# A two-block transformer kernel on one core: 256-byte lines, four query heads at a time, a third raw panel buffer, and five moves in the order of work

## The chip, the cores and the metric

The kernel runs on one core of one Trainium2 chip. The metric is device time in microseconds (us) of one execution; lower is better. TensorE (PE) does the matmuls, VectorE (DVE) and ScalarE (ACT) the elementwise work, GpSimd (POOL) a few small operations, and all DMAs are issued from SyncE's queue (SP).

## The reference

Everything is float32. `first_block` runs two layers over 512 tokens of width 1024. Each layer has a mixing part and a feed-forward part:

```python
h = rmsnorm(x, g_pre_mix[l])
(c_q, c_kv, k_r, p_in, s_u, s_v, cv_b, cv_c, cv_x, gate_logits) = split_cols(h @ w_in[l])
y_a = mla_branch(c_q, c_kv, k_r, ...) @ w_br_a[l]      # 8 heads, latent attention
y_b = pool_branch(p_in, ...) @ w_br_b[l]
y_c = sgu_branch(s_u, s_v, ...) @ w_br_c[l]
y_d = conv_branch(cv_b, cv_c, cv_x, ...) @ w_br_d[l]
merged = sum of sigmoid(gate_logits)[branch] * y_branch
x = x + rmsnorm(merged @ w_out[l], g_post_mix[l])
h = rmsnorm(x, g_pre_ffn[l])
x = x + rmsnorm((silu(h @ w_ffn_gate[l]) * (h @ w_ffn_up[l])) @ w_ffn_down[l], g_post_ffn[l])
```

`second_block` runs one layer: a modulated norm, neighbourhood attention with 8 heads, a gated linear attention in both directions (which also reads 256 context tokens), output gates, a merge, `w_out`, and a feed-forward part of the same shape.

## The kernel before

**Matmuls.** A float32 product is made of three matmuls in the fp32r type: `split` casts an operand into a high part on ACT (L261) and makes the low part, the rest, on DVE (L262), and `mm3` (L309) adds high x high, high x low and low x high in one PSUM bank. In the trace `wh` and `wl` are the two parts of a weight panel, `hTh` and `hTl` those of the transposed activations, `ah`/`al`, `mTh`/`mTl`, `brh`/`brl`, `oTh`/`oTl` those of other operands. In `out<-a,b` the first input is the one that streams, the second the one that is loaded as weights.

**Weight panels.** `panel` (L273) loads 128 x 1024 floats with one DMA into a raw buffer `wr` (two of them, `WR`), then splits it into `wh` and `wl` (four of each, `WH`). A raw buffer is free again when its `wl` is made; a `wh`/`wl` pair when the last matmul that reads it is done. Where four panels are used for all four token tiles in turn (`tm`, L574, called with the list that `pans` makes), a new set of four can be split only as the last tile releases the old set.

**Order.** TensorE's order is the program's: `inorder` (L245) chains every matmul to the one before. The other engines' order is made by the tile framework's scheduler from the program order and its own estimate of when inputs are ready; each engine then runs its list strictly in order, the DMA queue as well. Side work is woven in by hand: `beside` (L188) takes a list of items, and a `tick` (L153), twice per full matmul group, runs one step of it; `later(f, n)` runs `f` at the n-th tick from then.

**PSUM.** The eight banks are tagged `g` (3), `s` (2), `tp` (2), `po` (1). The main thread takes `g` for everything, side work takes `s` for products and `tp` for transposes.

**SBUF.** Pools are stacks, one growing from the left and one from the right. `Aligned.tile` (L100) rounds a tile's row up to a multiple of 128 bytes, so a tile may start at an odd multiple of 128. In the first block a pool `const1` stays open under all stage pools on the left; its tiles of 34, 4, 12 and 8 floats take 256 + 128 + 128 + 128 = 640 bytes, an odd number of 128-byte lines, and its one other tile 2048. It is closed before the second block.

**Places that the change touches.**
- `mla` (L735): `queries(hp, t2)` projects two heads for two token tiles: 12 matmuls of 192 columns (L764), four head transposes and a copy. There are eight calls per layer. `keys` and `scores` go by pairs of heads; the item list is at L831.
- `sgu_branch`: `turned` (L944) transposes two groups of four 128 x 128 tiles into `g` banks, and `split` empties them.
- `ffn_up` (L479): six panels lead, two of them made ahead of time. They run on the first 256 tokens while the pending transposes of token tiles 2 and 3 (`flush`) are placed after panels 1 and 3. The four other leading panels' `wl` are queued on DVE behind the split of tile 1.
- `block2` (L1114): neighbourhood queries, then the gated linear attention's inputs (panel set at column 1536), context tiles, the set at 2048, the sets for neighbourhood keys (512) and values (1024), and then four panels at 2560 for the output gates `og` (L1183), each made just before its matmuls. `on_v` issues eight DMAs per token tile.
- `normed` (L1496): the norm of neighbourhood queries and keys; its transposes come three ticks later.
- `norm` (L350) of the context tiles, and `decays` (L1277), take scratch tiles of their own.

Of the kernel before, what the change touches and what calls it, by code (L numbers as in the profile page):

```python
# [24 lines left out]
EPS = 1e-6  # L25
NEG = -1e30
HEADS = 8
WR, WH = 2, 4
F2 = {"g": 4, "a": 4}
LEAD = 6  # L30
TURN = 2
# [7 lines left out]
WIN0 = (0, 8, 24, 32)  # L39
CTX = 256  # L40
PHASE = 0
WARM = 12
HIGH = ((0, 0), (1, 0), (0, 1))

# [49 lines left out]
class Aligned:  # L94
# [5 lines left out]
    def tile(self, shape, dt, **kw):  # L100
        size = 2 if dt == BF16 else 4
        n = math.prod(shape[1:])
        if n * size % P == 0:
            return self.pool.tile(shape, dt, **kw)
        line = P // size
        t = self.pool.tile([shape[0], -(-n // line) * line], dt, **kw)[:, :n]
        if len(shape) == 2:
            return t
        names = "abc"[: len(shape) - 1]
        spaced = " ".join(names)  # L110
        return t.rearrange(f"p ({spaced}) -> p {spaced}", **dict(zip(names[1:], shape[2:])))


class Builder:
# [232 lines left out]
        lo = pool.tile([P, KD, n], F32R, name=self.nm("hTl"), tag="hTl")  # L347
        return hi, lo

    def norm(self, q, x, g, b=None, after=None):  # L350

        nc = self.nc
        ms = self.small(1)
        j = q.tile([P, D], BF16, name=self.nm("jk"), tag="jk")
        self.queue(nc.scalar.activation(j, x, AF.Square, scale=D ** -0.5, accum_out=ms), after)  # L355
        r = self.rstd(ms, 1)
        hns = []
        for h in range(2):
            c = slice(h * 512, h * 512 + 512)
            hn = q.tile([P, 512], F32, name=self.nm("hn"), tag="hn", bufs=4)  # L360
# [118 lines left out]
    def ffn_up(self, hT, before, wg, wu, ks, rs):  # L479
        nc = self.nc  # L480
        acts = []
        jobs = [(i, w) for i in range(NFF) for w in (wg, wu)]
        pans = self.ahead + [self.panel(w, 0, KD, i * P, P, after=self.turned_at[1] if i < 2 else None) for i, w in jobs[len(self.ahead) : LEAD]]
        banks = [self.bank(x) for x in ("g", "g", "g", "po", "s", "s")]

        def part(n, h):
            ts = slice(h * 256, h * 256 + 256)
            if n == h == 0:
                ls, rs = ([(x[0][:, k, c], x[1][:, k, c]) for k in range(KD)] for x, c in ((pans[0], slice(P)), (hT, ts)))
                return self.mm3s(banks[0][:, ts], ls, rs, HIGH)  # L490
            for k in range(KD):
                self.mm3(banks[n][:, ts], (pans[n][0][:, k], pans[n][1][:, k]), (hT[0][:, k, ts], hT[1][:, k, ts]), k == 0, k == KD - 1)

        for n in range(LEAD):
            part(n, 0)
            if n in (1, 3):
                self.flush()
        for n in range(LEAD):
            part(n, 1)
        before.close()  # L500
        keep = self.pool("actk", 1, stack=ks)
        drop = self.pool("actd", 1, stack=rs, side="right")
# [232 lines left out]
    def mla(self, l, o, q, kv):  # L735
# [19 lines left out]
        def queries(hp, t2):  # L755
            if t2 == 0:
                wqs[hp] = self.panel(a["w_uq"][l], 0, 2, hp * 192, 192)
                qTs[hp] = q.tile([QK, 2, SEQ], F32, name=self.nm("qT"), tag="qT", bufs=2)
            wq, qT = wqs[hp], qTs[hp]
            ps = self.ps()  # L760
            for i in range(2):
                ts = slice((2 * t2 + i) * P, (2 * t2 + i) * P + P)
                for k in range(2):
                    self.mm3(ps[:, i * 192 : i * 192 + 192], (cT[0][:, k, ts], cT[1][:, k, ts]), (wq[0][:, k], wq[1][:, k]), k == 0, k == 1)  # L764
            four = lambda x, d: x.rearrange("p (t h d) -> p t h d", t=2, h=2)
            v = four(ps[:, :384], QK)
            qn = self.f2()
            qv = four(qn[:, :384], QK)
            nc.scalar.activation(qv[:, :, :, :64], v[:, :, :, :64], AF.Copy, scale=QK ** -0.5)
            rt = self.f2()  # L770
            ra, rb = four(rt[:, :128], ROPE), four(rt[:, 128:256], ROPE)
            tab = lambda x, lo, hi: x[:, 2 * t2 : 2 * t2 + 2, None, lo:hi].to_broadcast([P, 2, 2, hi - lo])
            nc.vector.tensor_tensor(ra, v[:, :, :, 64:96], tab(Cq, 0, 32), op=ALU.mult)
            nc.vector.tensor_tensor(rb[:, :, :, :16], v[:, :, :, 80:96], tab(Sq, 0, 16), op=ALU.mult)
            nc.vector.tensor_tensor(rb[:, :, :, 16:], v[:, :, :, 64:80], tab(Sq, 16, 32), op=ALU.mult)
            nc.vector.tensor_tensor(qv[:, :, :, 64:96], ra, rb, op=ALU.add)

            def turn():
                pt = self.ps("t")
                for i in range(4):  # L780
                    self.transpose(pt[:QK, i * P : i * P + P], qv[:, i // 2, i % 2], ident)
                nc.scalar.copy(qT.rearrange("p h (t n) -> p t h n", t=NT)[:, 2 * t2 : 2 * t2 + 2], pt[:QK].rearrange("p (t h n) -> p t h n", t=2, h=2))

            pTs["q", hp, t2] = turn

        def keys(hp):
            wk = self.panel(ukv, 0, 1, hp * 256, 256)
# [9 lines left out]
        def scores(hp, j):  # L797
            n = (j + 1) * P
            ps = []
            for i in range(2):  # L800
                s = self.ps()
                self.matmul(s[:, :n], qTs[hp][:, i, j * P : j * P + P], kTs[hp][:, i, :n], start=True, stop=True)
# [22 lines left out]
        def do(f, *args):  # L825
            return lambda: f(*args)

        def project(hp):
            return [[do(queries, hp, t2), lambda: None, lambda t2=t2: pTs.pop(("q", hp, t2))()] for t2 in range(2)] + [[do(keys, hp)]]

        items = [[do(values, t)] for t in range(NT)] + project(0) + [[]]  # L831
        for hp in range(4):
            more = project(hp + 1) if hp < 3 else []
            for j in range(NT):
                items.append([do(scores, hp, j), lambda: None, do(probs, hp, j), do(values_of, hp, j)])
                if more:
                    items.append(more.pop(0))
        return items

    def softmax(self, q, s, n, bufs):  # L840
# [64 lines left out]
    def sgu_branch(self, l, w_in, hT, brp, q):  # L905
# [37 lines left out]

        def turned():  # L944
            for m in range(2):
                pt = self.ps("t")
                for t in range(NT):
                    self.transpose(pt[:, t * P : (t + 1) * P], cs[:, t, m * P : (m + 1) * P], ident)
                self.split(cT[0][:, m], cT[1][:, m], pt)
# [164 lines left out]
    def block2(self, hT, before):  # L1114
# [24 lines left out]
        with ExitStack() as st:  # L1139
            tmp = self.pool("ctx", 1, stack=st, side="right")  # L1140
            A, B = self.mod_rows(2)(tmp, "ga"), self.mod_rows(5)(tmp, "gb")
            with self.thread("a"):
                for t in range(2):
                    xc = tmp.tile([P, D], F32, name=self.nm("xc"), tag=f"xc{t}")
                    nc.sync.dma_start(xc, a["ctx_2"][0, t * P : (t + 1) * P])
                    hns = self.norm(tmp, xc, A, B)
# [21 lines left out]
        for name, c0 in (("k", 512), ("v", 1024)):  # L1168
            pans = self.pans(w_in, c0)
            for h, n, nt in ((hcT, name + "c", 2), (hT, name, NT)):  # L1170
                for t in range(nt):
                    ps = self.tm(h, pans, t, 512)
                    with self.thread("a"):
                        na[n](t, ps)
        self.drain()
# [4 lines left out]
        og = [q.tile([P, SEQ], F32, name=self.nm("og"), tag=f"og{m}") for m in range(4)]  # L1180
        self.beside(self.gla_outputs(gla, og, zT, q), 1)
        for m in range(4):
            ps = self.fm(hT, self.panel(w_in, 0, KD, 2560 + m * P, P), 0)  # L1183
            nc.scalar.activation(og[m], ps, AF.Tanh, scale=0.5)
            nc.vector.scalar_tensor_tensor(og[m], og[m], 1.0, ps, op0=ALU.add, op1=ALU.mult)
            nc.vector.tensor_scalar(og[m], og[m], gla["gain"], 0.5, op0=ALU.mult, op1=ALU.mult)
# [43 lines left out]
    def gla_project(self, hT, q, cq):  # L1230
# [46 lines left out]
        def decays(tmp):  # L1277

            jobs = [(zc, t, lac) for t in range(2)] + [(zT, t, la) for t in range(NT)]
            es, ds = ([tmp.tile([P, 512], F32, name=self.nm("g" + x), tag=f"g{x}{i}") for i in range(6)] for x in "ed")  # L1280

            def finish(i):
                t, dst = jobs[i][1:]
# [198 lines left out]
    def na_project(self, q):  # L1482
# [13 lines left out]
        def normed(ps, turned):  # L1496
# [15 lines left out]
            self.later(turn, 3)  # L1512

        def on_k(t, ps):
            dst = kT[:, :2048].rearrange("p (i n) -> p i n", i=4)[:, :, t * P : t * P + P]
# [150 lines left out]
```

## Time and profile before

| | us |
|---|---|
| median of 3 runs | 2477.08 (2476.04 to 2478.45) |
| the profiled execution's own time | 2477.62 |
| its span, first to last instruction | 2475.8 |
| mean granted TensorE clock | 0.996 of full |

| engine | busy us | share | instructions |
|---|---|---|---|
| PE | 2450.2 | 99% | 12155 |
| weight loads (PEld) | 2017.2 | 81% | 12155 |
| DVE | 1232.1 | 50% | 2018 |
| ACT | 851.2 | 34% | 1414 |
| POOL | 73.4 | 3% | 113 |

Matmuls are pipelined: one is listed with 0.39 us, but the next starts long before that. What a matmul costs is the distance from its start to the next one's start, and a stretch with a known number of matmuls shows how much of it was lost.

### The profile page before, as it was taken

To read this page: it belongs to the slowest core of one execution; us is meant where nothing else is said; L and a number is where in the kernel's file an instruction comes from. 1 tells how busy PE (TensorE), PEld (TensorE's weight loads), DVE (VectorE), ACT (ScalarE), POOL (GpSimd) and SP (SyncE) were. 2 spreads that over 40 slices of the span, in tenths; PEclk is the share of its full clock that TensorE was granted. 3 is DMA by queue.
4 is the path that set the end of the run, shared out by engine and by line. 5 is a ranking of instruction groups with operands and counts; after the bars stand their busy time and mean duration, and the time that the engine had idled before them with its cause. 6 is when DMAs were issued, how large, how long until landed. Compare 5 with 4: busy or idle time off the path is not lost.

```text
span 2475.8 us, 30539 instructions
## 1 busy us (share of the span) xinstructions
PE 2450.2 (99%) x12155; PEld 2017.2 (81%) x12155; DVE 1232.1 (50%) x2018; ACT 851.2 (34%) x1414; POOL 73.4 (3%) x113
## 2 busy tenths in 40 slices
PE   9999999999999999999999999999999999999999
PEld 7877788988888887778898888877877778988887
DVE  6456544566522645554455443275535646543323
ACT  4343433322322434343332222244434533322211
POOL 1000000000000100000000000020100000000000
PEclk9999999999999999999999999999999999999999
DMA  5323334345424432443435333451133225333323
GB/s 160 92 75 110 105 94 153 119 136 174 134 94 141 128 96 79 123 124 94 153 111 154 101 96 104 141 179 48 55 94 120 69 69 170 111 94 97 99 94 128
DMA packets 339376, 279.72 MB, mean 113 GB/s; under 512 B 28262, under 2 KB 282430, under 8 KB 339233
## 3 DMA queue, kind: packets, MB, share of 16 engines
q1 hardware_dynamic: 339233, 277.76, 37.6%
q8 instruction: 96, 1.57, 0.3%
q14 instruction: 47, 0.39, 0.0%
HBM read 262.27 MB, written 15.45 MB: 112 GB/s over the span
## 4 chain that ended last, share of the span: by engine, by line
PE 61%; DVE 3%; ACT 1%; issue 1%; DMA 1%; POOL 0%; DVEq 0%; ACTq 0%; POOLq 0%; SPq 0%
PE pg L252 47%; PE ps L252 6%; PE ppo L252 3%; PE ptp L252 3%; PE ptp L255 2%; DVE wl L262 1%; DMA wr<-in_w_mod 1%; ACT wh L261 0%; POOL sm L337 0%; DVE hn L361 0%; ACT p L847 0%; DVE xt L412 0%; DVE hTl L262 0%; ACT jk L355 0%; DMA wr<-in_w_ffn_up 0%
## 5 line engine op out<-in xcount | busy, mean ns | idle before, releaser
L262 DVE TENSOR_TENSOR wl<-wr,wh 128x1024 fp32r<-128x1024 f32 (+1 forms) x392 | 463.6, 1184 | 739.2 <-ACT wh L261 719.1
L261 ACT CAST wh<-wr 128x1024 fp32r<-128x1024 f32 (+1 forms) x392 | 398.9, 1020 | 1063.3 <-issue 394.4
L252 PE MATMUL pg<-hTh,wh 128*128 128x512 f32 x1760 | 693.7, 394 | 3.2 <-ACT wh L261 2.1
L252 PE MATMUL pg<-hTh,wl 128*128 128x512 f32 x1760 | 682.3, 388 | 0.3 <-DVE wl L262 0.3
L252 PE MATMUL pg<-hTl,wh 128*128 128x512 f32 x1760 | 681.6, 387 | 0.0
L252 PEld LDWEIGHTS pg<-hTh,wh 128*128 128x128 f32 x1760 | 331.3, 188 | 75.5 <-issue 6.4
L252 PEld LDWEIGHTS pg<-hTh,wl 128*128 128x128 f32 x1760 | 331.1, 188 | 69.8 <-DVE wl L262 1.1
L252 PEld LDWEIGHTS pg<-hTl,wh 128*128 128x128 f32 x1760 | 331.5, 188 | 67.4 <-issue 2.4
L252 PE MATMUL pg<-wh,hTh 128*128 128x512 f32 (+2 forms) x288 | 113.6, 396 | 1.2 <-ACT wh L261 1.2
L252 PE MATMUL pg<-wl,hTh 128*128 128x512 f32 (+2 forms) x288 | 110.9, 387 | 3.3 <-DVE wl L262 3.3
L337 POOL TENSOR_TENSOR sm<-sm,misc 128x1 f32<-128x1 f32 (+3 forms) x72 | 58.8, 819 | 1745.2 <-DVE sm L336 1032.2
L252 PE MATMUL pg<-wh,hTl 128*128 128x512 f32 (+2 forms) x288 | 110.1, 384 | 0.0
L512 DVE TENSOR_TENSOR f<-f,pg 128x512 f32<-128x512 f32 x60 | 41.2, 686 | 122.0 <-PE pg L252 121.9
L1078 DVE SCALAR_TENSOR_TENSOR f<-wr,misc,f 128x512 f32<-128x512 f32 x112 | 81.3, 747 | 29.6 <-DMA wr<-in_w_mod 29.1
L847 ACT ACTIVATE p<-ps,sm 128x512 f32<-128x512 f32 (+3 forms) x96 | 55.7, 580 | 89.6 <-DVE sm L844 89.6
L252 PE MATMUL pg<-wh,al 128*128 128x512 f32 x198 | 77.3, 390 | 0.0
L252 PE MATMUL pg<-wl,ah 128*128 128x512 f32 x198 | 77.3, 390 | 0.0
L252 PE MATMUL pg<-wh,ah 128*128 128x512 f32 x198 | 77.3, 390 | 0.0
L252 PEld LDWEIGHTS pg<-wl,hTh 128*128 128x128 f32 x288 | 54.5, 189 | 16.2 <-DVE wl L262 6.0
L252 PEld LDWEIGHTS pg<-wh,hTh 128*128 128x128 f32 x288 | 54.5, 189 | 12.4 <-ACT wh L261 2.1
L252 PEld LDWEIGHTS pg<-wh,hTl 128*128 128x128 f32 x288 | 54.5, 189 | 10.2
L859 ACT COPY pT<-ptp 128x512 f32<-128x512 f32 (+3 forms) x96 | 41.5, 484 | 50.3 <-PE ptp L255 50.2
(361 smaller groups left out, 3605.7 us busy)
## 6 DMA issues: line engine op xcount, KB each, us to landing
wr<-in_w_in SPq DMA_DIRECT2D x128, 512.0 KB
wr<-in_w_ffn_gate SPq DMA_DIRECT2D x66, 512.0 KB
wr<-in_w_ffn_up SPq DMA_DIRECT2D x66, 512.0 KB
wr<-in_w_ffn_down SPq DMA_DIRECT2D x66, 512.0 KB
wr<-in_w_mod SPq DMA_DIRECT2D x96, 256.0 KB
wr<-in_w_out SPq DMA_DIRECT2D x24, 512.0 KB
xd<-xt SPq DMA_DIRECT2D x20, 512.0 KB
xt<-xd SPq DMA_DIRECT2D x20, 512.0 KB
```

The lines of the kernel that those rows point to most:

```text
L252: self.inorder(self.nc.tensor.matmul(*args, **kw))
L255: self.inorder(self.nc.tensor.transpose(*args, **kw))
L261: h = (copy or nc.scalar.copy)(hi, src)
L262: l = nc.vector.tensor_tensor(lo, src, hi.bitcast(F32), op=ALU.subtract)
L337: nc.gpsimd.tensor_tensor(r, r, self.mhalf[:, :n], op=ALU.pow)
L512: nc.vector.tensor_tensor(t, t, ps, op=ALU.mult)
L847: nc.scalar.activation(p[:, :n], s[:, :n], AF.Exp, bias=nm, accum_out=sm)
L859: self.nc.scalar.copy(pT[:, :n], tp[:, :n])
L1078: nc.vector.scalar_tensor_tensor(acc, raw, sc, acc, op0=ALU.mult, op1=ALU.add)
```

## The change

- `WR` goes from 2 to 3: a third raw panel buffer.
- `LINE = 256`: tiles are rounded up to 256 bytes instead of 128.
- `queries` takes four heads and one token tile per call: 6 matmuls of 384 columns. There are still eight calls per layer; `qT` is twice as large. The item list is rearranged: keys of pair 1 in the first pair's scores, queries of heads 4 to 7 and keys of pair 2 in the second's, keys of pair 3 in the third's.
- `sgu_branch.turned` takes `tp` banks.
- `ffn_up`: only four leading panels at first; the other two after the first `flush`, with their `wl` queued behind the split of token tile 2.
- `block2`: the four output-gate panels are asked for after the matmuls of the last value tile.
- Neighbourhood queries' transposes come five ticks later instead of three; keys keep three.
- The context norm writes over its input, the sixth `ds` tile of `decays` is taken from the thread's scratch buffers, and the DMA scratch is 512 instead of 1024.

```diff
-WR, WH = 2, 4
+WR, WH = 3, 4
+LINE = 256
...
-        if n * size % P == 0:
+        if n * size % LINE == 0:
...
-        line = P // size
+        line = LINE // size
...
-        pans = self.ahead + [self.panel(w, 0, KD, i * P, P, after=self.turned_at[1] if i < 2 else None) for i, w in jobs[len(self.ahead) : LEAD]]
+        pans = list(self.ahead)
+
+        def more(n):
+            for i, w in jobs[len(pans) : n]:
+                pans.append(self.panel(w, 0, KD, i * P, P, after=self.turned_at[1]))
+
+        more(LEAD - 2)
...
             if n in (1, 3):
                 self.flush()
+                more(LEAD)
...
-            for i in range(2):
-                ts = slice((2 * t2 + i) * P, (2 * t2 + i) * P + P)
-                for k in range(2):
-                    self.mm3(ps[:, i * 192 : i * 192 + 192], (cT[0][:, k, ts], cT[1][:, k, ts]), (wq[0][:, k], wq[1][:, k]), k == 0, k == 1)
+            for k, w in enumerate(wqs[f]):
+                self.mm3(ps[:, :384], (cT[0][:, k, ts], cT[1][:, k, ts]), (w[0][:, 0], w[1][:, 0]), k == 0, k == 1)
...
-        items = [[do(values, t)] for t in range(NT)] + project(0) + [[]]
+        items = [[do(values, t)] for t in range(NT)] + project(0) + [[do(keys, 0)], []]
+        more = [[[do(keys, 1)]], project(1) + [[do(keys, 2)]], [[do(keys, 3)]], []]
...
-                pt = self.ps("t")
+                pt = self.bank("tp")
...
                     ps = self.tm(h, pans, t, 512)
+                    if n == "v" and t == NT - 1:
+                        pans = [self.panel(w_in, 0, KD, 2560 + m * P, P) for m in range(4)]
...
-            ps = self.fm(hT, self.panel(w_in, 0, KD, 2560 + m * P, P), 0)
+            ps = self.fm(hT, pans[m], 0)
...
-            normed(ps, turned)
+            normed(ps, turned, 5)
```

## Rows read from the trace of the kernel before

**Rows 1.** The page, part 1: busy us, share, instructions of each engine.
```profile
PE 2450.2 (99%) x12155; PEld 2017.2 (81%) x12155; DVE 1232.1 (50%) x2018; ACT 851.2 (34%) x1414; POOL 73.4 (3%) x113
```

**Rows 2.** The page, part 4: the chain that ended last, shares by engine.
```profile
PE 61%; DVE 3%; ACT 1%; issue 1%; DMA 1%; POOL 0%; DVEq 0%; ACTq 0%; POOLq 0%; SPq 0%
```

**Rows 3.** Timeline of PE (start, us, instruction): a query burst, a value burst.
```profile
106.91 0.25 PE L252 MATMUL ps<-wh,cTh 128*128 128x192 f32 x1
...
108.23 0.42 PE L252 MATMUL pg<-hTh,wh 128*128 128x512 f32 x1
...
62.19 0.28 PE L252 MATMUL ps<-wh,cTh 128*128 128x256 f32 x1
...
62.90 0.39 PE L252 MATMUL pg<-hTh,wh 128*128 128x512 f32 x1
```

**Rows 4.** Groups by form, PE (count, busy us, mean ns, idle): two gate products.
```profile
L252 PE MATMUL pg<-brl,wh 128*128 128x512 f32 x96 | 37.8, 394 | 0.0
...
L252 PE MATMUL pg<-oTl,wh 128*128 128x512 f32 x96 | 37.3, 389 | 0.0
```

**Rows 5.** Timeline of PE: one down projection, before and after its operands change pool.
```profile
772.51 0.39 PE L252 MATMUL ps<-wh,ah 128*128 128x512 f32 x1
...
794.28 0.40 PE L252 MATMUL ps<-wh,ah 128*128 128x512 f32 x1
...
808.92 0.40 PE L252 MATMUL ptp<-wh,ah 128*128 128x512 f32 x1
```

**Rows 6.** Timeline of PE: output projection of block 1 and of block 2.
```profile
415.16 0.39 PE L252 MATMUL pg<-wh,mTh 128*128 128x512 f32 x1
...
433.99 0.40 PE L252 MATMUL ps<-wh,mTh 128*128 128x512 f32 x1
...
2063.22 0.39 PE L252 MATMUL pg<-wh,mTh 128*128 128x512 f32 x1
...
2084.30 0.39 PE L252 MATMUL ps<-wh,mTh 128*128 128x512 f32 x1
```

**Rows 7.** Windows, PE: stretch, length, busy (matmuls touched), granted clock, DMA share, GB/s.
```profile
1691.03:1702.56 11.53, 8.71 (x27) 0.85 0.59 150
1730.98:1738.07 7.09, 5.37 (x21) 1.00 0.63 185
1829.29:1839.15 9.86, 7.40 (x25) 0.65 0.41 106
```

**Rows 8.** The chain in order of time, 1726 to 1740 us (start, us, what).
```profile
1729.90 4.53 DMA wr<-in_w_in
...
1735.53 1.24 DVE wl L262
```

**Rows 9.** Timeline of ACT, around 1830 us.
```profile
1830.47 0.60 ACT L1413 ACTIVATE f<-ps 128x512 f32<-128x512 f32 x1
1830.95 2.00 ACT L261 CAST wh<-wr 128x1024 fp32r<-128x1024 f32 x2
```

**Rows 10.** Timeline of PE, end of the gating unit in layer 1 (idle before, releaser).
```profile
295.80 1.03 PE L255 MATMUL pg<-ident,su 128*128 128x128 f32 x8
297.36 0.50 PE L252 MATMUL pg<-hTh,wh 128*128 128x512 f32 x1 [0.53 <-ACT f L659]
```

**Rows 11.** Timeline of PE: fourth tile's transposes in both feed-forward parts of block 1.
```profile
460.90 0.66 PE L255 MATMUL ptp<-ident,hn 128*128 128x128 f32 x4 [0.34 <-DVE hTl L262]
...
1267.95 0.66 PE L255 MATMUL ptp<-ident,hn 128*128 128x128 f32 x4 [1.37 <-DVE hTl L262]
```

**Rows 12.** Timeline of DVE, 1264 to 1268 us.
```profile
1264.52 0.68 DVE L262 TENSOR_TENSOR hTl<-ptp,hTh 128x512 fp32r<-128x512 f32 x1
1266.07 1.23 DVE L262 TENSOR_TENSOR wl<-wr,wh 128x1024 fp32r<-128x1024 f32 x1 [0.87 <-ACT wh L261]
1267.21 1.28 DVE L262 TENSOR_TENSOR hTl<-ptp,hTh 128x512 fp32r<-128x512 f32 x2
```

**Rows 13.** Timeline of PE, start of block 2.
```profile
1642.52 0.66 PE L255 MATMUL ptp<-ident,hn 128*128 128x128 f32 x4 [0.79 <-ACT nqT L1529]
```

More of the change, by code (lines that the diff above doesn't have):

```diff
@@ L348, in alloc_hT, with norm @@
         return hi, lo
-    def norm(self, q, x, g, b=None, after=None):
+    def norm(self, q, x, g, b=None, after=None, over=False):
         nc = self.nc
@@ L359, in norm @@
             c = slice(h * 512, h * 512 + 512)
-            hn = q.tile([P, 512], F32, name=self.nm("hn"), tag="hn", bufs=4)
+            hn = x[:, c] if over else q.tile([P, 512], F32, name=self.nm("hn"), tag="hn", bufs=4)
             nc.vector.scalar_tensor_tensor(hn, x[:, c], r, g[h] if isinstance(g, list) else g[:, c], op0=ALU.mult, op1=ALU.mult)
@@ L753, in values, with queries @@
             nc.scalar.copy(V[:, t], ps)
[L755 to L759, printed above, removed]
-            ps = self.ps()
-            for i in range(2):
-                ts = slice((2 * t2 + i) * P, (2 * t2 + i) * P + P)
-                for k in range(2):
-                    self.mm3(ps[:, i * 192 : i * 192 + 192], (cT[0][:, k, ts], cT[1][:, k, ts]), (wq[0][:, k], wq[1][:, k]), k == 0, k == 1)
-            four = lambda x, d: x.rearrange("p (t h d) -> p t h d", t=2, h=2)
+        def queries(f, t):
+            if t == 0:
+                wqs[f] = [self.panel(a["w_uq"][l], k, 1, f * 384, 384) for k in range(2)]
+                qTs[f] = q.tile([QK, 4, SEQ], F32, name=self.nm("qT"), tag="qT", bufs=2)
+            qT = qTs[f]
+            ts = slice(t * P, t * P + P)
+            ps = self.ps()
+            for k, w in enumerate(wqs[f]):
+                self.mm3(ps[:, :384], (cT[0][:, k, ts], cT[1][:, k, ts]), (w[0][:, 0], w[1][:, 0]), k == 0, k == 1)
+            four = lambda x, d: x.rearrange("p (h d) -> p h d", h=4)
             v = four(ps[:, :384], QK)
@@ L768, in queries @@
             qv = four(qn[:, :384], QK)
-            nc.scalar.activation(qv[:, :, :, :64], v[:, :, :, :64], AF.Copy, scale=QK ** -0.5)
+            nc.scalar.activation(qv[:, :, :64], v[:, :, :64], AF.Copy, scale=QK ** -0.5)
             rt = self.f2()
             ra, rb = four(rt[:, :128], ROPE), four(rt[:, 128:256], ROPE)
[L772 to L776, printed above, removed]
+            tab = lambda x, lo, hi: x[:, t, None, lo:hi].to_broadcast([P, 4, hi - lo])
+            nc.vector.tensor_tensor(ra, v[:, :, 64:96], tab(Cq, 0, 32), op=ALU.mult)
+            nc.vector.tensor_tensor(rb[:, :, :16], v[:, :, 80:96], tab(Sq, 0, 16), op=ALU.mult)
+            nc.vector.tensor_tensor(rb[:, :, 16:], v[:, :, 64:80], tab(Sq, 16, 32), op=ALU.mult)
+            nc.vector.tensor_tensor(qv[:, :, 64:96], ra, rb, op=ALU.add)
             def turn():
@@ L780, in turn @@
                 for i in range(4):
-                    self.transpose(pt[:QK, i * P : i * P + P], qv[:, i // 2, i % 2], ident)
-                nc.scalar.copy(qT.rearrange("p h (t n) -> p t h n", t=NT)[:, 2 * t2 : 2 * t2 + 2], pt[:QK].rearrange("p (t h n) -> p t h n", t=2, h=2))
-            pTs["q", hp, t2] = turn
+                    self.transpose(pt[:QK, i * P : i * P + P], qv[:, i], ident)
+                nc.scalar.copy(qT[:, :, ts], pt[:QK].rearrange("p (h n) -> p h n", h=4))
+            pTs["q", f, t] = turn
         def keys(hp):
@@ L801, in scores @@
                 s = self.ps()
-                self.matmul(s[:, :n], qTs[hp][:, i, j * P : j * P + P], kTs[hp][:, i, :n], start=True, stop=True)
+                self.matmul(s[:, :n], qTs[hp // 2][:, 2 * (hp % 2) + i, j * P : j * P + P], kTs[hp][:, i, :n], start=True, stop=True)
                 nc.vector.memset(s[:64, n - 64 : n], NEG)
@@ L826, in do, with project @@
             return lambda: f(*args)
-        def project(hp):
-            return [[do(queries, hp, t2), lambda: None, lambda t2=t2: pTs.pop(("q", hp, t2))()] for t2 in range(2)] + [[do(keys, hp)]]
-        items = [[do(values, t)] for t in range(NT)] + project(0) + [[]]
+        def project(f):
+            return [[do(queries, f, t), lambda: None, lambda t=t: pTs.pop(("q", f, t))()] for t in range(NT)]
+        items = [[do(values, t)] for t in range(NT)] + project(0) + [[do(keys, 0)], []]
+        more = [[[do(keys, 1)]], project(1) + [[do(keys, 2)]], [[do(keys, 3)]], []]
         for hp in range(4):
-            more = project(hp + 1) if hp < 3 else []
             for j in range(NT):
                 items.append([do(scores, hp, j), lambda: None, do(probs, hp, j), do(values_of, hp, j)])
-                if more:
-                    items.append(more.pop(0))
+                if more[hp]:
+                    items.append(more[hp].pop(0))
+            items += more[hp]
         return items
@@ L1145, in block2 @@
                     nc.sync.dma_start(xc, a["ctx_2"][0, t * P : (t + 1) * P])
-                    hns = self.norm(tmp, xc, A, B)
+                    hns = self.norm(tmp, xc, A, B, over=True)
                     self.later(lambda t=t, hns=hns: self.turn(hns, hcT, t), 8 + t)
@@ L1279, in decays @@
             jobs = [(zc, t, lac) for t in range(2)] + [(zT, t, la) for t in range(NT)]
-            es, ds = ([tmp.tile([P, 512], F32, name=self.nm("g" + x), tag=f"g{x}{i}") for i in range(6)] for x in "ed")
+            es, ds = ([tmp.tile([P, 512], F32, name=self.nm("g" + x), tag=f"g{x}{i}") for i in range(n)] for x, n in (("e", 6), ("d", 5)))
+            ds.append(self.f2())
             def finish(i):
@@ L1494, in na_project, with normed @@
         vd = self.dp.tile([NT, 2, P, 512], F32, name="vd")
-        def normed(ps, turned):
+        def normed(ps, turned, n=3):
             sq = self.f2()
@@ L1510, in turn @@
                 turned(pt)
-            self.later(turn, 3)
+            self.later(turn, n)
         def on_k(t, ps):
@@ L1644 @@
     from concourse.bass_utils import run_bass_kernel_spmd
-    nc = bacc.Bacc("TRN2", target_bir_lowering=False, num_devices=1, dynamic_dma_scratch_size=1024)
+    nc = bacc.Bacc("TRN2", target_bir_lowering=False, num_devices=1, dynamic_dma_scratch_size=512)
     arrays, aps = {}, {}
```

## The prediction

> **What bounds the kernel now.** I read the page's busy times first: PE is busy in 99% of the span [rows 1], and the chain that ended last is PE's more than anything else's [rows 2]. No other engine is above half. So an edit is worth what it takes out of TensorE's stream: fewer or shorter matmuls, or a stop of that stream that goes away. The timeline then gives the true price of a matmul, the distance between starts: in the second half of a down projection 96 matmuls of 512 columns start between 772.51 and 794.28 us, 0.2268 us each [rows 5]. With that price every stretch can be checked: length less count x price is loss. Going through the stream in this way I find eight stops that an edit of this change aims at; the three large ones are in one windows table [rows 7], the others carry their own idle time [rows 10, 11, 13].
>
> **The change part by part.** Sums are made against the profiled execution's own 2477.62 us.
>
> *Four heads.* Twelve 192-column matmuls take 108.23 - 106.91 = 1.32 us, 0.110 each [rows 3]; a layer has 8 such bursts, so 2 x 8 x 12 = 192 matmuls cost 21.1 us. They become 96 of 384 columns, a width that the trace does not have. Below, the 256-column price: six in 62.90 - 62.19 = 0.71, 0.118 each [rows 3], 11.4 us in all; above, the 512-column price, 21.8 us. 384 is half way between, so I take half way, 0.1725 each: 16.6 us. Gain 4.5, bounds +9.7 and -0.7. Transposes, copies and rotations stay eight of each per layer with the same sizes, and run on engines with half their time free; the panels stay four per layer with as many floats, and SP's queue gets none more. Keys of pair 2 now come one step ahead of their scores instead of two; a step is some 4 us of PE work and the copies behind it fit in that.
>
> [...]
>
> *Lines of 256 bytes.* In one loop of the down projection, same code, same banks, the price changes when its operand `ah` passes from the pool on the right to the one on the left: 63 matmuls between 794.28 and 808.92 us are 0.2324 each against 0.2268 before [rows 5]. The left pool lies above `const1`, whose 640 bytes put it at an odd multiple of 128. The output projection repeats it: in block 1, 81 matmuls between 415.16 and 433.99 us, 0.2325 each; in block 2, with `const1` closed, 93 between 2063.22 and 2084.30, 0.2267 [rows 6]. After the change those four tiles take 4 x 256 bytes and all of this lies on even lines. Each is 5.7 ns dear: 2 layers x 192 matmuls of the last eight `ah` plus 2 x 192 of `mT` are 768, 4.4 us. The branch products `br` lie there too (394 against 389 ns for `oT` on the right, [rows 4]): 288 x 5 ns = 1.4. Gain 5.8; at worst, if the place in a line isn't the reason, 0.
>
> [...]
>
> *Third raw buffer.* Where one set of four panels follows another, panels 3 and 4 are loaded only when 1 and 2 have been split: the chain shows 4.53 us of DMA and then the split [rows 8]. The stretch 1730.98 to 1738.07 holds 20 matmul starts (21 touch it): 7.09 - 20 x 0.227 = 2.55 lost [rows 7]. With three buffers panel 3 is there, and panel 4's load begins when panel 1 is split, as panel 3's did, alone on the queue: all 2.55 go. [...] Gain 6.25, bounds 8.2 and 0. Late next is DVE's list. Elsewhere panels are ahead of PE already and nothing is gained.
>
> *Output-gate panels.* The stretch 1829.29 to 1839.15 has four 256-column matmuls (0.47), twelve of 512 (2.72) and eight transposes (1.0 as in [rows 10]): 4.2 of 9.86 us; 5.7 are lost, at a mean clock of 0.65 [rows 7]. ACT casts the third and fourth panel only after the gated attention's exponentials [rows 9]. Asked for before the last value tile's copy, all four can be split while PE still runs value tile 3 and gate 1. On SP's queue the four loads pass eight of the value tiles' DMAs, whose reader, the attention, comes much later; on ACT one 0.59 copy may sit behind a 1.05 cast, which three `g` banks cover. Gain 5.7; nothing if SP holds the fourth load behind the value DMAs, but one panel later at most.
>
> *Gating unit's banks.* After its eight transposes PE waits 0.53 us for a `g` bank [rows 10], alike in layer 2: 1.06. With `tp` banks the next group has its three. Bounds: +1.06, and -1.0 if the transposes have to wait for a probability copy in `tp`.
>
> *Leading panels.* Tile 3's second half waits 0.34 and 1.37 us for the `tp` bank that tile 2's second half still holds [rows 11]; DVE puts a panel's `wl` between tile 2's halves [rows 12]. Behind that turn, both halves are split together: gain 1.7. The two `wl` (1.23 each) then come later, needed some 1.3 us after the turn, and behind them on DVE stands only tile 3's split, which PE reads three panels later; bounds +1.7 and -1.2 per feed-forward part, -3.6.
>
> *Later query turns.* Four query transposes take a `tp` bank just ahead of tile 3's, which wait 0.79 us for the copies out of it [rows 13]. Two ticks later they are out of the way: gain 0.8.
>
> *The context norm in place, the scratch tile and the DMA scratch* change only where data lies: 0. The in-place write follows the square that reads the same tile, as its copy did.
>
> Sum: 4.5 + 5.8 + 6.25 + 5.7 + 1.1 + 1.7 + 0.8 = 25.9. 2477.62 - 25.9 = 2451.7; the median of the runs is 0.54 below the profiled execution, so **2451 us** after rounding.
>
> **Rivals.**
> (a) *Price of a matmul not as read*: the shift by 128 bytes isn't what costs 5.7 ns, or the 384-column matmul isn't below the 512-column one. For it: both are seen only together with other things (another pool, another loop). Against it: [rows 5] change in mid-loop. Without 5.8 and with half of the 4.5: 2451 + 8 = 2459. [...] Chance 13%: 7% for the line alone, 4% for the query price alone, 2% for both.
> (b) *The waits move on*: DVE's list or the DMA queue, which the scheduler orders anew, is late where the panels were; the three stretches of [rows 7] keep half, 6 us, and the leading panels give back 2: 2459. For it: [rows 12] show one split of 1.23 us holding up the two behind it. Against it: DVE is at 50%. Chance 15%; both (a) and (b), 2467, 3%.
> (c) *More goes than aimed at*: a third buffer also takes panel loads off the queue ahead of other DMAs, and stops that I left alone shrink: 2445. Chance 8%.
> (d) *Slower: the stage changes*. 4 KB for raw buffers and 8 KB for queries on the left shift what each newly opened pool lies on; a pool laid over tiles still in use has to wait, and PE stops at a stage change with no panel ready, at the price of [rows 7], 5.7 us. Six tails and the stage changes of block 2 could show it; from five such stops on it eats the 25.9, with six the time is 2451 + 34 = 2485. Against it: the left-hand neighbours of a new pool are mostly long done. Chance 3%.
> (e) *Nothing*: the scheduler undoes the moves in order and the prices are as in (a): 2477 within 4. Chance 3%.
>
> **How the numbers follow.** The forecast has 55%, with 2446 to 2457 as its own range. The whole range takes in (a) and (b) singly and stops short of both and of (d): 2444 to 2466. What a measurement of this kernel can tell from no change is about 0.2%, 5 us, so faster means under 2472. Faster: forecast, (a), (b), both and (c), 94%. Within 0.2%: (e), 3%. Slower: (d), 3%.
>
> **What would show it.** 48 query matmuls of 128x384 per layer at about 0.173 us between starts; `mTh`, `brh` and late `ah` matmuls in block 1 at 0.227 instead of 0.2325; no idle time at the three stretches of [rows 7] beyond some 2 us, and a clock of 1.0 there; no `ACT f L659`, `DVE hTl` and `ACT nqT` behind PE's idle times of [rows 10, 11, 13]. If the 512-column matmuls of block 1's output projection still take 0.2325, the line term is wrong; if PE's busy share falls, (b) or (d) is at work. A time over 2466 would mean that prices and waits both went wrong.

## The result, and the profile after

The changed kernel takes **2456.74 us** (median of 4 runs, 2455.86 to 2458.86) against 2477.46 of the kernel before in the same session: a ratio of 0.9918, 95% interval 0.9901 to 0.9935. The forecast was 2451, range 2444 to 2466. The profiled executions, on which the sum was made, stand at 2455.86 against 2477.62: 21.8 us less where 25.9 were forecast. Some 4 us of the sum did not come.

The page of the changed kernel, PE's part of part 1 and the shares of part 4, against [rows 1, 2]:

```profile
PE 2432.2 (99%) x12059; PEld 2008.6 (82%) x12059; DVE 1232.5 (50%) x2018; ACT 849.4 (35%) x1414; POOL 75.6 (3%) x113
...
PE 91%; DVE 4%; DMA 1%; ACT 1%; issue 1%; POOL 1%; ACTq 0%; DVEq 0%; POOLq 0%; SPq 0%
```

PE is still what bounds it, with 96 matmuls less. PE has most of the chain that ended last in both; its shares can't be set side by side, since all shares of the kernel before add up to 67% of the span and those of the changed kernel to 99%. The windows of the changed kernel from the same matmul to the same matmul as the three stretches of [rows 7] (after the times: length, then busy time of PE, PEld, DVE, ACT, POOL, PE's granted clock, DMA share and GB/s):

```profile
1679.26:1687.11 7.85, 6.96 (x27) 4.57 (x26) 6.86 (x9) 4.19 (x8) 0.00 (x0) 1.00 0.68 187
1715.48:1720.37 4.89, 4.82 (x22) 3.68 (x21) 1.47 (x2) 2.33 (x2) 0.00 (x0) 1.00 0.86 272
1811.58:1815.59 4.01, 4.01 (x25) 3.47 (x24) 2.29 (x4) 1.73 (x4) 0.00 (x0) 1.00 0.25 75
```

11.53, 7.09 and 9.86 us have become 7.85, 4.89 and 4.01: 3.7, 2.2 and 5.9 less, and the clock, which had a mean of 0.85 and 0.65 in two of them, is 1.00 in all. That is what the sum had for them. Part of it is the clock of this one execution of the kernel before: with two buffers and a clock of 1.00 the first stretch takes 10.27 us (kernel without the third buffer, below), so that 2.4 of the 3.7 are the panels and 1.3 the clock. What the sum did not have are waits that are new. Timeline of PE (start, us, instruction; in brackets the idle time before it and its releaser):

```profile
817.08 1.32 PE L256 MATMUL ptp<-ident,hn 128*128 128x128 f32 x8 [1.14 <-DVE hn L362]
...
1039.90 0.50 PE L253 MATMUL pg<-wl,hTh 128*128 128x512 f32 x1 [1.11 <-DVE wl L263]
...
1618.68 0.66 PE L256 MATMUL ptp<-ident,hn 128*128 128x128 f32 x4 [0.55 <-DVE fg L404]
...
1627.39 1.03 PE L256 MATMUL ptp<-ident,hn 128*128 128x128 f32 x8
...
1633.85 0.50 PE L253 MATMUL pg<-ah,hTl 128*128 128x512 f32 x1 [2.24 <-DVE hTl L263]
...
1880.79 0.50 PE L253 MATMUL ps<-nk,nq 64*128 64x512 f32 x1 [0.48 <-ACT p L856]
1882.45 0.97 PE L253 MATMUL ps<-nk,nq 64*128 64x512 f32 x5 [1.16 <-ACT p L856]
```

The fourth token tile's eight transposes at 1627.39 now run without the wait of [rows 13]. (Where the tiles are counted from 0, as in most of the expectations, this one is the third.) Of the new waits, the ones before 1880 are put down to DVE. Its timeline near 816 and near 1633:

```profile
811.26 3.09 DVE L263 TENSOR_TENSOR wl<-wr,wh 128x832 fp32r<-128x832 f32 x3
814.27 1.28 DVE L263 TENSOR_TENSOR hTl<-pg,hTh 128x512 fp32r<-128x512 f32 x2
...
816.27 1.41 DVE L362 SCALAR_TENSOR_TENSOR hn<-xt,sm,g 128x512 f32<-128x512 f32 x2
```

```profile
1626.50 1.22 DVE L263 TENSOR_TENSOR wl<-wr,wh 128x1024 fp32r<-128x1024 f32 x1
1629.26 0.69 DVE L1516 TENSOR_TENSOR f<-pg,sm 128x512 f32<-128x512 f32 x1 [1.54 <-POOL sm L338]
...
1632.51 0.69 DVE L1516 TENSOR_TENSOR f<-pg,sm 128x512 f32<-128x512 f32 x1 [1.76 <-POOL sm L338]
1633.11 1.28 DVE L263 TENSOR_TENSOR hTl<-ptp,hTh 128x512 fp32r<-128x512 f32 x2
```

Near 811 three low parts of panels stand in a row before the split and the norm that the next transposes need. Near 1630 the fourth tile's split has had its transposes since 1628.4, and stands behind two norms of neighbourhood queries, which wait 1.54 and 1.76 us for POOL.

Where the time went, by the start of the same matmul in the two profiled executions (forecast: the prediction's terms that lie in the stretch; the layers' terms are halved between the layers):

| up to (before -> after) | measured | forecast |
|---|---|---|
| layer 1's output projection, 415.16 -> 410.44 | -4.7 | -3.5 |
| its last down projection, 808.92 -> 802.00 | -2.2 | -2.5 |
| layer 2's start, 826.03 -> 820.14 | **+1.0** | 0 |
| the last down projection of layer 2, 1620.93 -> 1606.87 | -8.2 | -7.1 |
| neighbourhood queries, 1660.01 -> 1647.72 | **+1.8** | -0.8 |
| panel change, 1702.58 -> 1687.11 | -3.2 | -3.7 |
| panel change, 1738.08 -> 1720.37 | -2.2 | -2.5 |
| output gates, 1839.16 -> 1815.59 | -5.9 | -5.7 |
| first neighbourhood scores, 1915.00 -> 1892.32 | **+0.9** | 0 |
| the end, 2477.62 -> 2455.86 | +0.9 | 0 |

The last line is the executions' own time. It holds no wait of a matmul: the last matmul starts at 2470.42 and 2447.67, 22.7 us earlier, and the 0.9 lies behind it.

### The profile page after: what moved, and what is told of

Its sections match the earlier page's. It is cut to its first block, busy times and chain, and to the rows that moved or that the text cites. A ratio compares the mean times of both kernels' runs of the same rounds, so it can differ in the third digit from the quotient of the medians.

```text
span 2454.1 us, 30336 instructions
## 1 busy us (share of the span) xinstructions
PE 2432.2 (99%) x12059; PEld 2008.6 (82%) x12059; DVE 1232.5 (50%) x2018; ACT 849.4 (35%) x1414; POOL 75.6 (3%) x113
## 3 DMA queue, kind: packets, MB, share of 16 engines
q8 instruction: 95, 1.56, 0.3%
## 4 chain that ended last, share of the span: by engine, by line
PE 91%; DVE 4%; DMA 1%; ACT 1%; issue 1%; POOL 1%; ACTq 0%; DVEq 0%; POOLq 0%; SPq 0%
PE pg L253 69%; PE ps L253 9%; PE ppo L253 5%; PE ptp L253 5%; PE ptp L256 3%; DMA wr<-in_w_mod 1%; DVE wl L263 1%; POOL sm L338 1%; ACT wh L262 1%; DVE f L1087 1%; DVE hn L362 0%; DVE fg L404 0%; ACT p L856 0%; PE ps L256 0%; PE pg L256 0%
```

## The experiments

Differences between kernels of one group are given by their ratios to the kernel before, times 2476 us. Each ratio is uncertain by about 0.0014, 3.5 us, so a verdict rests on the rows of the trace and the time only has to agree.

**Lines.** The kernel before, everything on the left of block 1 moved by 128 bytes:

```diff
+        cp.tile([P, 32], F32, name="shift")
         self.rope = cp.tile([P, 4, NT, ROPE], F32, name="rope")
```

> The kernel before with one tile of 32 floats more in const1 and nothing else: every pool on the left of the first block moves up by 128 bytes, from an odd to an even multiple. If the place in a 256-byte line is what makes the late ah, mT and br matmuls of block 1 cost 0.2325 us instead of 0.2268, they all go to 0.227 and the time falls by 5.8 us, to about 2471.5 (ratio 0.9977). If the place does not matter, and the price came from the loop or the pool, the time stays at 2477.5 and mTh keeps 0.2325 us between starts. If the shift makes other tiles odd that were even, the gain is smaller than 5.8.

2471.7 against 2475.4 us, ratio 0.9986 (0.9977 to 0.9995): 3.7 us less, 1.2 to 5.7. The timeline of PE has the same matmuls as [rows 5, 6]:

```profile
791.70 0.39 PE L252 MATMUL ps<-wh,ah 128*128 128x512 f32 x1
...
805.98 0.39 PE L252 MATMUL ptp<-wh,ah 128*128 128x512 f32 x1
...
412.75 0.39 PE L252 MATMUL pg<-wh,mTh 128*128 128x512 f32 x1
...
431.11 0.39 PE L252 MATMUL ps<-wh,mTh 128*128 128x512 f32 x1
```

63 matmuls in 14.28 us and 81 in 18.36: 0.2267 each, where they took 0.2324 and 0.2325. In the groups by form `brl` falls from 394 to 390 ns. Nothing else was changed, so the move by 128 bytes is the cause. The changed kernel has the same price (18.36 us from 410.44 to 428.80). By these figures the operands' matmuls cost 768 x 0.0058 + 288 x 0.004 = 5.6 us less. The whole need not show all of that, because waits move: where [rows 11] have 0.34, the fourth tile's transposes now wait longer for DVE,

```profile
458.92 0.66 PE L255 MATMUL ptp<-ident,hn 128*128 128x128 f32 x4 [1.47 <-DVE hTl L262]
```

and near 821, at layer 2's start, PE waits 0.53 us where the kernel before waits 0.20.

**Four heads.** The changed kernel with `queries`, `project` and the item list of the kernel before (its lines are in the diff ahead):

> The changed kernel with the queries of the kernel before (two heads, two token tiles, 12 matmuls of 192 columns) and its item list. By the traces of both kernels the 192 matmuls of 192 columns took 22.0 us from start to start and the 96 of 384 columns 18.0: 4.0 us above the changed kernel, if nothing else hangs on it. [...] A loss of more than 5 would mean that the new item list was worth something by itself.

2461.6 us, ratio 0.9936 (0.9924 to 0.9949); the changed kernel itself, run again in this group, 2457.45, 0.9920 (0.9906 to 0.9934), with its waits in the same places:

> The changed kernel itself, as the measure for the other three of this group on the same chip: a ratio of 0.9918 to the kernel before within 0.001, with the same waits of TensorE near 816, 1618, 1633 and 1881 us.

So two heads cost 4.0 more by the ratios, which alone would not be clear of their uncertainty; the bursts of the traces have to show it. Timeline of PE, a burst of the changed kernel, and then one of the two-head kernel:

```profile
89.88 0.42 PE L253 MATMUL ps<-wh,cTh 128*128 128x384 f32 x1
90.14 0.33 PE L253 MATMUL ps<-wl,cTh 128*128 128x384 f32 x1
...
91.02 0.39 PE L253 MATMUL pg<-hTh,wh 128*128 128x512 f32 x1
```

```profile
107.13 0.25 PE L253 MATMUL ps<-wh,cTh 128*128 128x192 f32 x1
...
108.45 0.41 PE L253 MATMUL pg<-hTh,wh 128*128 128x512 f32 x1
```

Six of 384 columns take 1.14 us (1.07 to 1.15 in the 16 bursts, 17.9 in all). Twelve of 192 take 1.32 in this burst and in five others, and 1.40 in the other ten, 21.9 in all (22.0 in the kernel before): 4.0 us, as the ratios have it. The wait of 1.11 us near 1040 belongs to this part, too: every traced kernel with four heads has it with 0.8 to 1.1, and those with two heads have at most 0.3 there. In return PE's two waits for the softmax's `p` in layer 2, 0.83 and 1.14 near 1057 in the kernel before, are 0.52 and 0.20 near 1029 in the changed one.

**What the third raw buffer does.** Five kernels: the changed one without it, the kernel before with it alone, and the changed one without one of three other edits each.

```diff
-WR, WH = 3, 4
+WR, WH = 2, 4
```

> The changed kernel with two raw panel buffers again, all else kept. Theory: the third buffer took 6.5 us out of the panel changes of 1691 and 1731 us of the kernel before, but it also lets the scheduler put panels' low parts earlier in VectorE's list, in front of the norms and splits that TensorE waits for at the starts of layer 2 and of block 2, which gives back 4 to 5 us. Then this kernel loses 6.5 and wins 4 to 5: 2458 to 2459 us; TensorE's waits of 1.1 us near 816, 0.55 near 1618 and 2.2 near 1633 us of the changed kernel are gone, those at the two panel changes are back with 2.5 and 5.6. Rival: those three waits come from the later query turns and the other moves; they stay, and the time is 2463.

2459.95 us, ratio 0.9938 (0.9925 to 0.9950): 4.5 above the changed kernel's 0.9920. Its windows from the same matmuls:

```profile
1679.16:1689.43 10.27, 7.37 (x28) 4.57 (x26) 7.02 (x9) 4.28 (x8) 0.00 (x0) 1.00 0.55 153
1717.80:1725.04 7.24, 5.44 (x21) 3.60 (x20) 2.45 (x2) 3.38 (x3) 0.00 (x0) 1.00 0.63 183
1816.59:1820.60 4.01, 4.01 (x25) 3.47 (x24) 2.29 (x4) 1.73 (x4) 0.00 (x0) 1.00 0.75 212
```

The two panel changes are 2.4 and 2.35 longer again, the gates are not. Of the new waits the one of 1.14 near 816 has become 0.61, the one near 1618 is gone, and at the fourth tile's split PE waits 0.31 us:

```profile
1633.72 0.50 PE L253 MATMUL pg<-ah,hTl 128*128 128x512 f32 x1 [0.31 <-DVE hTl L263]
```

The theory holds for the waits near 1618 and 1633 and for half of the one near 816; the other half stays without the buffer, and the shifted kernel, with two buffers, has 0.53 there as well. The panel changes cost 4.8 us, not 6.5, at a clock of 1.00. The price of going without the buffer is larger than expected all the same, since PE also has idle times of 0.35 and 0.24 us near 1242 and 1258 us, at the start of layer 2's feed-forward part, where the changed kernel has none; that part's start is 1.5 us longer in all. On DVE two low parts stand before the split near 816, not three:

```profile
812.45 1.96 DVE L263 TENSOR_TENSOR wl<-wr,wh 128x832 fp32r<-128x832 f32 x2
814.32 1.28 DVE L263 TENSOR_TENSOR hTl<-pg,hTh 128x512 fp32r<-128x512 f32 x2
```

The third buffer alone, in the kernel before (`WR = 3`, and the in-place norm, scratch tile and DMA scratch of the change to make room):

> The kernel before with the third raw buffer and what makes room for it (context norm in place, one scratch tile, the smaller DMA scratch), and nothing else. By the prediction's terms: the 6.25 us of the two panel changes go and the 5.7 at the output gates stay: 2471. If the third buffer by itself lets the gate panels be split in time, the gates' wait is gone too, 12 in all, and the waits that its order of VectorE's list makes (1.0 near layer 2's start, 3 near the neighbourhood queries, 1 at their scores) take back 5: 2470, with no wait at the gates.

2471.49 against 2475.82 us, ratio 0.9980 (0.9972 to 0.9989). Its windows, then PE's timeline:

```profile
1695.21:1703.06 7.85, 6.94 (x28) 4.58 (x26) 6.84 (x9) 4.19 (x8) 0.00 (x0) 1.00 0.67 187
1731.45:1736.46 5.01, 4.83 (x22) 3.68 (x20) 1.47 (x2) 2.33 (x2) 0.00 (x0) 1.00 0.82 267
1827.68:1831.70 4.02, 4.02 (x26) 3.47 (x24) 3.19 (x5) 2.67 (x5) 0.00 (x0) 1.00 0.12 29
```

```profile
460.09 1.04 PE L255 MATMUL ptp<-ident,hn 128*128 128x128 f32 x8
...
1267.16 1.03 PE L255 MATMUL ptp<-ident,hn 128*128 128x128 f32 x8
...
1643.26 0.63 PE L255 MATMUL ptp<-ident,f 128*128 128x128 f32 x4 [2.55 <-DVE f L1505]
...
2114.78 1.25 PE L255 MATMUL ptp<-ident,hn 128*128 128x128 f32 x8 [0.91 <-DVE hTl L262]
```

The buffer by itself clears the gates, and the fourth tile's turn runs through in both layers (eight transposes in one row, where [rows 11] have a wait of 0.34 and 1.37 in the middle). It also makes new waits, 2.55 and 0.91 us here. The stretch of the first of them, 1637.06 to 1660.00 us of the kernel before, is 4.3 us longer, more than the wait: the granted clock has a mean of 0.94 in it, against 1.00.

The gate panels asked for late again:

```diff
-                    if n == "v" and t == NT - 1:
-                        pans = [self.panel(w_in, 0, KD, 2560 + m * P, P) for m in range(4)]
...
-            ps = self.fm(hT, pans[m], 0)
+            ps = self.fm(hT, self.panel(w_in, 0, KD, 2560 + m * P, P), 0)
```

> The changed kernel with the four output-gate panels asked for one by one again, just before their matmuls; three raw buffers stay. If the move of the panels is what took away the 5.7 us at the output gates, all of it comes back. If the third raw buffer does most of it, because the scheduler can then load and split three of the panels ahead by itself, only the fourth panel is late: 0 to 2.5 us.

2457.61 us, ratio 0.9920 (0.9907 to 0.9934), and no wait at the gates:

```profile
1814.85:1818.86 4.01, 4.01 (x26) 3.47 (x25) 3.42 (x5) 2.86 (x6) 0.00 (x0) 1.00 0.03 7
```

With two buffers the early request is enough, with three it is not needed. Likewise the leading panels, all four asked for at once:

```diff
-        pans = list(self.ahead)
...
-        more(LEAD - 2)
+        pans = self.ahead + [self.panel(w, 0, KD, i * P, P, after=self.turned_at[1] if i < 2 else None) for i, w in jobs[len(self.ahead) : LEAD]]
```

> The changed kernel with all four leading panels of the feed-forward part asked for at once again, two of them with their low parts behind the split of token tile 1. The waits of TensorE between the halves of the third tile's turn come back with 0.5 and 1.5 us, as in the kernel before: 2 us above the changed kernel, ratio 0.9928. If they stay away, the third raw buffer or the new lines had already cured them.

2456.87 us, ratio 0.9920 (0.9906 to 0.9933): the expected waits do not come back. They stay away in both layers, and one of 0.91 us comes in block 2's feed-forward part:

```profile
454.42 1.04 PE L256 MATMUL ptp<-ident,hn 128*128 128x128 f32 x8
...
1253.84 1.03 PE L256 MATMUL ptp<-ident,hn 128*128 128x128 f32 x8
...
2099.60 1.25 PE L256 MATMUL ptp<-ident,hn 128*128 128x128 f32 x8 [0.91 <-DVE hTl L263]
```

The query turns at three ticks again:

```diff
-            normed(ps, turned, 5)
+            normed(ps, turned)
```

> The changed kernel with the neighbourhood query transposes three ticks later again instead of five. Theory (the third buffer's order of VectorE's list makes the wait of 2.2 us near 1633): the wait for the copies ahead of the third tile's turn comes back with about 0.9 us, and the wait for the low parts behind it shrinks by as much but stays at 1.3 or more: 2456.7 within 1. Rival (the later turns make that wait): it goes altogether, 2455.2.

2458.84 us, ratio 0.9934 (0.9922 to 0.9947), 3.5 above the changed kernel's ratio. Neither number was right: the late DVE list now meets the query transposes themselves.

```profile
1630.27 1.09 PE L256 MATMUL ptp<-ident,f 128*128 128x128 f32 x4 [2.57 <-DVE f L1516]
...
1632.59 1.11 PE L256 MATMUL ptp<-ident,hn 128*128 128x128 f32 x4 [0.38 <-ACT nqT L1541]
```

The later turns do not make the wait of 2.24; under three buffers they avoid a larger one. But the two waits are only 0.7 us more than 2.24. The rest is the clock: the windows of the changed kernel and of this one, from the wait of 0.55 near 1618 to the same matmul behind the queries,

```profile
1618.68:1655.01 36.33, 34.09 (x163) 27.36 (x163) 28.03 (x49) 16.91 (x37) 11.46 (x8) 1.00 0.55 174
...
1618.85:1658.77 39.92, 36.97 (x162) 29.61 (x163) 27.76 (x49) 17.69 (x39) 11.47 (x8) 0.91 0.52 162
```

differ by 3.6 us, and the granted clock has a mean of 0.91 in the second; from 1630 to 1636 us, behind the first of the two waits, it is 0.50, the lower of its two levels (the clock of the kernel before has 1.00 and 0.50 and nothing else, 0.50 among others from 1698.8 to 1702.2 and from 1831.9 to 1838.7 us). Whether it falls is not settled by the wait alone: the profiled executions of the kernels with the late gate request and with the early leading panels have the same wait of 2.25 us here, a clock of 0.93 and 1.6 us more than the changed kernel, which kept 1.00.

**A better order.** Two buffers up to the neighbourhood queries, a third from column 1536 on:

```diff
-WR, WH = 3, 4
+WR, WH = 2, 4
...
+            if self.th != "a" and self.third and self.nraw % 3 == 0:
+                raw = pool.tile([P, size], F32, name=self.nm("wr"), tag="wx", bufs=1)[:, :e]
...
+        self.third = True
         pans = self.pans(w_in, 1536)
```

> The changed kernel with two raw buffers until the neighbourhood queries are done, and the third from the panel set at column 1536 on, where the two panel changes are. Theory: the gains at the two panel changes stay (6.5 us), and the waits at the starts of layer 2 and block 2 go, 1.0 + 0.7 + 2.2 less some 0.2: 2453 us, 3.7 below the changed kernel. Rival (the third buffer has no part in those waits, or its early panel loads also helped the first block): 2456 to 2458.

2455.29 us, ratio 0.9920 (0.9906 to 0.9933): no gain, against the theory's 3.7. The wait near 1633 is 0.3, but a new one of 1.56 comes in layer 2's tail (timelines of DVE and PE):

```profile
1605.58 1.22 DVE L264 TENSOR_TENSOR ah<-wr,ah 128x1024 fp32r<-128x1024 f32 x1
1606.72 1.28 DVE L264 TENSOR_TENSOR hTl<-pg,hTh 128x512 fp32r<-128x512 f32 x2
```

```profile
1610.86 1.32 PE L257 MATMUL pg<-ident,hn 128*128 128x128 f32 x8 [1.56 <-DVE hn L369]
```

With two buffers the second lead panel of block 2 is split late and stands before the split and the norm. That is the smaller part of what is missing: from 1607 to 1624 us of the changed kernel the same work takes 0.45 us longer. The start of layer 2's feed-forward part (1240 to 1275 us) is 1.6 longer, much as in the kernel with two buffers throughout, and at the neighbourhood scores the clock fell in this execution. Windows of the changed kernel and of this one there, with the same waits:

```profile
1877.00:1892.32 15.32, 13.36 (x69) 9.28 (x67) 11.04 (x25) 6.79 (x16) 0.00 (x0) 1.00 0.38 105
...
1877.08:1894.01 16.93, 14.97 (x69) 10.45 (x67) 11.05 (x25) 6.80 (x16) 0.00 (x0) 0.90 0.35 94
```

Then with all three buffers, but the next low part (layer 2) or the next two (block 2) queued behind the fourth tile's split:

```diff
+        if self.th != "a" and self.hold:
+            self.hold -= 1
+            after = self.turned_at[1]
         load(raw)
...
+        self.hold = 1 if l else 0
...
+        self.hold = 2
         pans = self.pans(w_in, 1536)
```

> The changed kernel with all three raw buffers, but the low parts of one early panel in layer 2 and of two in block 2 (the set at 1536) are queued on VectorE behind the split of the third token tile. Theory (these low parts, which the third buffer lets in earlier, stand in front of the norms and splits that TensorE waits for): the waits near 816 (1.1 us) and 1633 (2.2 us) shrink to under 0.5 each, the one near 1618 (0.55, for a gated half that is queued behind a norm) may stay; 2.5 to 3.5 us below the changed kernel. Rival: something else in that list is late and the waits stay within 0.5 us of what they are; same time.

2455.08 us, ratio 0.9911 (0.9897 to 0.9924). The wait at 1633 is gone, the one near 816 is 0.61 and not under 0.5; others moved on, one of 0.87 to the split near 824 in layer 2, and here one to the narrow panel `lp` of the gated attention, whose split had come behind the two held ones:

```profile
1639.75 0.70 PE L254 MATMUL pg<-hTh,lp 128*96 128x512 f32 x2 [0.84 <-DVE lp L264]
```

So each low part gets the latest neighbour that it can bear: behind the third tile's norm in layer 2, behind `lp` in block 2 (`hn_at` holds the last instruction of each norm, `low` is the split of `lp`):

```diff
+            after = self.hold.pop()
...
+        self.hold = [self.hn_at[-2]] if l else []
...
+        self.hold = [low, low]
```

> The changed kernel with the low part of layer 2's first early panel queued on VectorE behind the norm of the third token tile, and the low parts of the first two panels of the set at 1536 behind that of the gated attention's narrow panel. The earlier trial put all three behind the split of the last tile and only moved half of the wait on (1.0 us each near 823 and 1638 us). Expected: no wait over 0.8 near 816 and none over 0.5 near 823, 1631 and 1638; 1.3 + 2.4 - 0.8 = 3 us below the changed kernel, ratio 0.9907. Rival: VectorE's list has no room left there and the waits move on again, ratio 0.991 or 0.992.

**2453.23 us**, ratio 0.9905 (0.9890 to 0.9920), the lowest median of all; by ratios 3.7 below the changed kernel run again, within the uncertainty of both. The trace has what was expected of the waits: layer 2's start is 0.55 us shorter than in the changed kernel, and the neighbourhood queries are 2.5 shorter. The profiled execution (2455.35, the longest of the four) gives 1.55 of it back at the neighbourhood scores, where its clock fell to a mean of 0.90. On DVE the low part of 1626.50 has left the list, the first query norm no longer waits, and the split comes in time, so that PE's timeline has no idle time from 1627 to 1634:

```profile
1626.38 0.68 DVE L1522 TENSOR_TENSOR f<-pg,sm 128x512 f32<-128x512 f32 x1
...
1629.62 0.69 DVE L1522 TENSOR_TENSOR f<-pg,sm 128x512 f32<-128x512 f32 x1 [1.76 <-POOL sm L341]
1630.23 1.28 DVE L264 TENSOR_TENSOR hTl<-ptp,hTh 128x512 fp32r<-128x512 f32 x2
```

## Why the prediction was right, and where it was not

*Four heads*: 4.5 forecast, 4.0 by the run. Both prices were read too low: the first of six takes 0.26 instead of 0.17 in most bursts, so that 384 columns cost 0.187 on the mean, not 0.1725; and the one burst of 192 columns that was read is one of the six short ones, so that the 192 matmuls cost 22.0 us, not 21.1: 0.115 each on the mean instead of 0.110. The two errors all but cancel.

*Lines*: 5.8 forecast; 0.0058 us less per matmul is shown, 5.6 by the matmuls, and the whole is 3.7 by the runs (1.2 to 5.7). That the place doesn't matter, the prediction's worst case with a gain of 0, does not agree with the shifted kernel.

*Third raw buffer*: 6.25 forecast for the two panel changes, 5.9 seen in the windows. Of the 6.25, 2.55 are for the second of them and 3.7 for the first; the 3.7 were the author's estimate, and no run shows the term as it was made: the first stretch went from 11.53 to 7.85 us, 3.7 less, of which 2.4 are the panels and 1.3 the clock. The step that failed is the last sentence of that part, that elsewhere "nothing is gained". Elsewhere the free buffer is used as well: the panel is loaded and cast earlier, and the scheduler then sets its low part earlier in DVE's list, before norms and splits that PE waits for. "Late next is DVE's list" was right, but at other places than the panel changes. New waits cost 1.0 at layer 2's start, 1.8 instead of -0.8 at the neighbourhood queries and 0.9 at their first scores, 4.5 in all. That the buffer makes about half of the first and nearly all of the second is shown by the kernels without it and by the held low parts; the other half of the first stays with two buffers. At the scores it is only seen that the buffer brings the longer wait, not through which instruction. That 4.5 is near the 4.1 that are missing is in part chance: 0.9 more came behind the last matmul, 0.9 in the other stretches of the table, and 2.3 went beyond the sum in the two layers. A part of these 2.3 is the lines: from 30 us to the output projection of layer 1 the shifted kernel is 1.7 us faster than the kernel before, where the sum had 0.7. The rest was not followed up.

*Output-gate panels* and *leading panels*: 5.7 and 1.7 forecast, both waits gone, but not by these edits alone. The third buffer by itself removes both, and in its presence the gate request is worth 0 and the leading panels 0.9 us of another wait. The sum came out right because each wait was counted once; that two edits aimed at the same wait was not seen. Of the sum, the buffer's part was mis-sized: with it alone go 5.8 + 5.8 + 1.7 (the windows, and [rows 11]), and 4.3 us by the medians are left after the new waits and the stretches at a lower clock behind them.

*Later query turns*: 0.8 forecast. The wait for the copies is gone. Under three buffers these two ticks are worth 3.5 by the ratios; in the traces 0.7 of it are waits, and the rest is the clock that fell in the kernel with three ticks.

*Gating unit's banks*: both waits of 0.53 are gone in the trace; not tried by itself.

Of the rivals, (b) is what happened in part: waits moved on, to places that it did not name. (a) is refuted by the shifted kernel and the two-head kernel. That the time still lies in the forecast's own range, 2446 to 2457, is in part luck: the buffer's gains at the gates and at the leading panels stood in the sum under other edits, and half of the 4.5 of new waits was made up by what the layers gained beyond the sum.

## What to carry to other kernels

A further buffer for loads is not only a gain where the loads are late: it also moves the work behind each load forward in the list of an engine that runs in order (on DVE the split near 1633 us had its transposes since 1628.4 and began at 1633.11), so look there for what the next wait needs, and queue that work explicitly behind it. When several edits could remove one wait, run each alone: here one buffer had already done what two other edits were for. Before a difference of 1 to 4 us between two traces is put down to an edit, compare the granted clock of the same stretch in both: here a fall of it was worth 1.3 to 3 us and came in some executions and not in others. And where a matmul's price changes in mid-loop with its operand's pool (here from 0.2268 to 0.2324 us), look at the operands' addresses first.

## What the runs showed of the hardware that was not expected

A 512-column fp32r matmul took 0.2325 us from start to start where its operand's tiles start at an odd multiple of 128 bytes (the kernel before), and 0.2267 at an even one (the shifted and the changed kernel). It shows for `ah` and `mT`, which are loaded as weights, and (390 against 394 ns in the groups) for `br`, which stream. Why is open: the records of the weight loads have 188 ns in both kernels.

The same wait of TensorE can leave the granted clock at 1.00 or be followed by a lower one, from one execution to the next. Behind the wait of 2.24 to 2.26 us near 1633 the clock stayed at 1.00 in both profiled executions of the changed kernel, and had a mean of 0.93 over the queries in those of the kernels with late gates, early leading panels and two heads, at a price of 1.6 us in the first two. What decides it no run here shows.
